# Blocks as the moving side in the compression's first layer, and decays as one product over 96 rows

## The chip, the cores and the metric

The kernel runs on one core of one Trainium2 chip. The metric is the time of the kernel on the device in microseconds (us). A core has a matrix engine (TensorE, PE in the profile; its weight loads are PEld), a vector engine (VectorE, DVE), a scalar engine (ScalarE, ACT), GpSimd (POOL), and SyncE (SP), which here issues the DMAs. Matrix products are written to PSUM, eight banks of 512 float32 columns on 128 partitions; everything else lies in SBUF.

## The reference, cut to what matters

One layer of a decoder over 1024 tokens of 1024 channels: two token mixers (native sparse attention and gated linear attention) read the same normalised input, then comes a gated feed-forward block. Two small pieces matter here. The sparse attention compresses keys and values in overlapping blocks of 32 tokens, 16 apart, for two groups, with a two-layer network:

```python
def compress_blocks(kv, pe, w1, w2):          # kv: (1, 2 groups, 1024, 64)
    ...                                       # 63 blocks of 32 x 64 for each group
    blocks = (blocks + pe).reshape(b, g, n_cmp, CMP_LEN * d)
    return jax.nn.silu(blocks @ w1) @ w2      # 2048 -> 128 -> 64
```

It is done once for keys and once for values. The linear attention has a decay for each token and key channel, from 16 numbers of low rank:

```python
log_a = jax.nn.log_sigmoid((lr_gla @ gla_gate_w2[layer] + gla_gate_b[layer])) / GLA_GATE_TAU   # 16 -> 256
```

## The kernel before

Activations lie channel-first: 128 channels on the partitions, tokens in the columns. Most products are made of two parts of each operand in float32r (a high part and what is left), as three matmuls; some small ones are plain float32, which the profile records as two passes for one matmul.

The program starts with a projection stage. `dense` turns jobs (a weight tile of 128 outputs and what to do with the result) into a list of small items, each of three matmuls for one of eight channel tiles (line 431), with items between that load the next weights: SP fetches them, ACT takes the high part (L372), POOL the rest (L373). Each job makes two halves of 512 tokens in PSUM banks of the kind `m`, of which there are two. The jobs are, in this order: a part of the linear attention's keys, `j0` (block keys), `key_job(0)` (rotated keys), `j1` (block values), `key_job(1)`. The order of the items is written out by hand in `fill.add(work[:7] + ...)`, and `fill.flush()` issues them in that order; the costs in the list play no part there. After them come two projections with tokens on the partitions (`token_proj`, L749 to L751): first `wb` (values of the linear attention), then `wa` (other values, gates and the 16 ranks `lr`). Then comes the recurrence of the linear attention (`gla_stream`, in 8 chunks), mixed with projections, and after it the attention, which a planner (`Plan`) arranges on TensorE by estimated times and in which L1210 turns the probabilities, then the merging and the feed-forward block.

TensorE runs in the order in which the program is written. The order on DVE, ACT, POOL and SP is fixed by the builder, which follows the program's order by a timeline of its own; a few stages set some of them by hand. A tile takes a free place of its kind and waits if there is none.

The compression is in `compress_job(kv)`. `fetch` loads w1 (2048 x 128 as 16 tiles), w2 and the positions. `evac` takes each half of the projection, scales it by `rbc` (the normalisation) on DVE into one tile `kst` for each group on partitions 0 to 63 (L641), and ACT copies it, shifted by one token, to partitions 64 to 127 (L644, L646), so that a column holds two neighbouring tokens. After the first half DVE also sums the positions times w1 into `pb` (L651, L653, sixteen operations). `hidden(g)` multiplies, for each of 16 pairs of places in the block, the 63 columns 16 apart (the standing side, loaded as weights) with the tile of w1 that belongs to the pair (the moving side) (L662); the second group's call adds `pb` (L666) and applies silu. Its result has the blocks on the partitions. `turned` turns it (L677, L680), and `second` makes the second layer (L686, L692).

The decays: `turn_rank(p)` turns the ranks of two token blocks on TensorE (L796), and DVE copies them to `lrT`, whose row 16 is one (L797). `decay(p)` multiplies them with `w2b`, 16 rows of weights and one of bias, in float32, one product for each block (L804), and takes the logarithm of the sigmoid. Pairs 0 and 1 are made in `token_proj(wa)`, pairs 2 and 3 in the recurrence, in chunks 1 and 3. `load_consts` loads `w2b` with the other constants.

Of the kernel before, what the change touches and what calls it, by code (L numbers as in the profile page):

```python
# [10 lines left out]
F32 = mybir.dt.float32  # L11
# [236 lines left out]
def layer_kernel(ctx, tc, a, outT):  # L248
# [86 lines left out]
    eps = cst.tile([128, 1], F32, name="eps")  # L335
    w2b = mcst.tile([17, 256], F32, name="w2b")

    def load_consts():
        load(ident, a["consts"][:, CI:CI + 128])
        load(tri, a["consts"][:, CTRI:CTRI + 128])  # L340
        load(cmul, a["consts"][:, CMUL:CMUL + 64])
        load(ggain, a["gla_norm"])
        load(w2b, a["gla_w2b"])
        V.tensor_copy(identb, ident)
        t = big("cst1")
        load(t[:, :512], a["consts"][:, CCMP:CCMP + 512])
        V.tensor_copy(cmb.rearrange("p b n -> p (b n)"), t[:, :512])
        t = big("cst2")
        load(t[:, :64 * NLV], a["consts"][:, CLEV:CLEV + 64 * NLV])
        V.tensor_copy(lev.rearrange("p b n -> p (b n)"), t[:, :64 * NLV])  # L350
# [272 lines left out]
    def compress_job(kv):  # L623
# [11 lines left out]
        def evac(p, hf):  # L635
            if hf == 0:
                d["s"] = [big("kst") for _ in range(NG)]
            for g in range(NG):
                r = slice(64 * g, 64 * g + 64)
                t, bc = d["s"][g], rbc[r, hs(hf)]  # L640
                V.tensor_mul(t[0:64, hs(hf)], p[r, :], bc)  # L641

                if hf == 0:
                    S.activation(t[64:128, 0:511], t[0:64, 1:512], AF.Copy)  # L644
                else:
                    S.activation(t[64:128, 511:1023], t[0:64, 512:1024], AF.Copy)  # L646

# [7 lines left out]

        def hidden(g):
            def fn():
                if g == 0:
                    d["ph"] = ps_m()
                dst = d["ph"][0:63, bs(g)]  # L660
                for j in range(16):
                    PE.matmul(dst, d["s"][g][:, 2 * j:2 * j + 993:16], d["w1"][j // 8][:, j % 8, :],  # L662
                              start=g + j == 0, stop=False)
                if g == 1:
                    for h in range(NG):
                        PE.matmul(d["ph"][0:63, bs(h)], ones[:, 0:63], d["b"], start=False, stop=h == NG - 1)  # L666
                    x, sg = d["h"], d["e"] = small("hx"), small("hs")
                    V.tensor_copy(x[0:63], d["ph"][0:63, :256])
                    log_sigmoid(sg[0:63], x[0:63])
                    S.activation(sg[0:63], sg[0:63], AF.Exp)  # L670
                    V.tensor_mul(x[0:63], x[0:63], sg[0:63])
            return fn

        def turned():
            ps = ps_m()
            for g in range(NG):
                PE.transpose(ps[:, 64 * g:64 * g + 63], d["h"][0:63, bs(g)], ident[0:63, 0:63])  # L677
            hd = d["hd"] = small("hd")
            P.memset(hd, 0.0)
            S.activation(hd[:, :128].rearrange("p (g n) -> p g n", g=NG)[:, :, 0:63],  # L680
                         ps[:, :128].rearrange("p (g n) -> p g n", g=NG)[:, :, 0:63], AF.Copy)

# [18 lines left out]

        return (a["w_t"][4 + kv], proj(evac)), [(2000.0, hidden(0)), (2000.0, hidden(1))], [(220.0, turned)], [(400.0, second)]

# [41 lines left out]
    def token_proj(parts, ncol, evac, after={}):  # L745
        for b in range(NB):
# [6 lines left out]
            for fn in after.get(b, []):  # L753
                fn()

    fetches = []
    j0, h0, t0, s0 = compress_job(0)
    j1, h1, t1, s1 = compress_job(1)
    lb, wb = token_weights(a["w_b"], 512, 2)
    work = dense([(a["w_t"][3], proj(lambda p, hf: scaled(kg[hf][:, 1, :], p, hf))), j0, key_job(0), j1, key_job(1)], ready=first)  # L760
    fill.add(work[:7] + [(900.0, first_roots), (0.0, load_consts), (0.0, fetches[0])] + work[7:20] + [(0.0, root_turned)] + work[20:48] + h0 + [(0.0, fetches[1])] + work[48:59] + t0
             + work[59:63] + s0 + work[63:69] + lb[:1] + work[69:74] + lb[1:2] + work[74:84] + h1 + lb[2:] + work[84:])
    fill.flush()
# [20 lines left out]
    la, wa = token_weights(a["w_a"], NA, 3)  # L784
    token_proj(wb, 512, evac_b, {0: [t1[0][1]], 2: [s1[0][1]], 4: [la[0][1]], 5: [la[1][1]], 6: [la[2][1]], 7: [la[3][1]]})


    lsg = [None] * 4
    lrT = [small("lrT") for _ in range(4)]
    for t in lrT:  # L790
        P.memset(t[0:32, :], 1.0)

    def turn_rank(p):
        ps = ps_t()
        for b in range(2):
            PE.transpose(ps[0:16, bs(b)], lr[:, 2 * p + b, :], ident)  # L796
        V.tensor_copy(lrT[p][0:16, :], ps[0:16, :256])  # L797

    def decay(p):
        z = mid("z")  # L800
        lsg[p] = mid("lsg", shape=(2, 256))
        ps = ps_d()
        for b in range(2):
            PE.matmul(ps[:, 256 * b:256 * (b + 1)], lrT[p][0:17, bs(b)], w2b, start=True, stop=True)  # L804
        S.activation(z, ps, AF.Copy)
        log_sigmoid(lsg[p].rearrange("p a b -> p (a b)"), z)
# [1144 lines left out]
```

## Time and profile before

| | us |
|---|---|
| runs, median (3 runs) | 1565.15 (1564.26 to 1566.31) |
| profiled execution, its own time | 1564.79 |
| span in its profile | 1563.0 |
| TensorE busy | 1542.0 |
| DVE busy | 1014.2 |
| ACT busy | 813.0 |
| POOL busy | 720.4 |

The profile is of one execution. The span goes from its first to its last instruction; the execution's own time has some us around it. An engine that is busy for nearly all of the span need not be at its best pace: matmuls are pipelined, and the start of one to the start of the next is what a matmul costs in a row of them. Rows of groups give: line, engine, operation, what is written from what, shapes, count, then busy time and mean of one, then the idle time ahead of them with what ended it. Rows of a timeline or a chain give: start, length, engine, line, operation, count. The granted clock of TensorE was 0.998 of full over the span.

### The profile page before, as it was taken

The page shows a single profiled execution, that of the slowest core. Times are in us where ns is not written, and L with a number is a line of the kernel's source. Part 1 is how long each engine was busy: PE and PEld are TensorE (multiplying, and loading weights), DVE is VectorE, ACT ScalarE, POOL GpSimd, SP SyncE. Part 2 cuts the span into 40 slices and gives each one's busy share as a digit, 9 for nine tenths or more (in the row PEclk, how much of TensorE's full clock was granted, in tenths as well). Part 3 has the DMA queues.
Part 4 walks back from the last instruction along what each step waited for, and adds up shares of the span by engine and source line. Part 5 has one row for each costly group of instructions (what it writes and reads, how often), then busy time and mean ns, then how long its engine had stood idle before and what let it go on. Part 6 is the DMA issues. An engine that isn't in the chain of part 4 may idle for free.

```text
span 1563.0 us, 22871 instructions
## 1 busy us (share of the span) xinstructions
PE 1542.0 (99%) x7871; PEld 1309.6 (84%) x7871; DVE 1014.2 (65%) x1788; ACT 813.0 (52%) x1615; POOL 720.4 (46%) x635
## 2 busy tenths in 40 slices
PE   9999999999999999999999999999999999999998
PEld 7888988888888888888888888888888888888887
DVE  7781487586787778777574677544444444599785
ACT  6241555575776767687653454334333334454542
POOL 6110366573223353343256510666666666555570
PEclk9999999999999999999999999999999999999999
DMA  5431212332111222221656621322222323885422
GB/s 180 139 105 55 69 51 65 119 108 78 48 58 55 77 87 72 85 88 61 200 169 229 197 88 68 121 101 102 101 101 102 101 101 108 299 320 163 141 88 108
DMA packets 109944, 180.15 MB, mean 115 GB/s; under 512 B 13426, under 2 KB 30595, under 8 KB 109828
## 3 DMA queue, kind: packets, MB, share of 16 engines
q1 hardware_dynamic: 105796, 172.25, 33.4%
q10 hardware_dynamic: 4032, 6.44, 1.1%
q8 instruction: 62, 1.02, 0.3%
q14 instruction: 54, 0.44, 0.1%
HBM read 128.57 MB, written 45.88 MB: 112 GB/s over the span
## 4 chain that ended last, share of the span: by engine, by line
PE 93%; DVE 3%; ACT 1%; issue 1%; POOL 0%; DVEq 0%; POOLq 0%; ACTq 0%
PE m L431 19%; PE d L431 11%; PE m L1494 9%; PE m L1492 9%; PE m L1493 9%; PE m L1880 5%; PE m L1882 4%; PE m L1881 4%; PE t L1210 3%; PE o L1219 3%; PE s L1130 2%; PE s L1129 2%; PE t L749 2%; PE t L750 1%; PE t L751 1%; PE t L884 1%
## 5 line engine op out<-in xcount | busy, mean ns | idle before, releaser
L373 POOL TENSOR_TENSOR wl<-wf,wh 128x512 fp32r<-128x512 f32 x106 | 146.5, 1389 | 260.7 <-ACT wh L372 237.4
L1492 PE MATMUL m<-xt,wh 128*128 128x512 f32 x412 | 160.3, 389 | 0.0
L1493 PE MATMUL m<-xt,wh 128*128 128x512 f32 x412 | 160.3, 389 | 0.0
L1494 PE MATMUL m<-xt,wl 128*128 128x512 f32 x412 | 160.3, 389 | 0.0
L1409 POOL TENSOR_TENSOR wl<-ws,wh 128x512 fp32r<-128x512 f32 x76 | 107.6, 1420 | 73.3 <-ACT wh L1408 73.3
L1188 DVE TENSOR_TENSOR ptl<-t,pth 128x512 fp32r<-128x512 f32 (+1 forms) x168 | 99.2, 597 | 42.7 <-ACT pth L1187 40.5
L1409 POOL TENSOR_TENSOR wl<-wr,wh 128x512 fp32r<-128x512 f32 x69 | 92.0, 1333 | 70.3 <-ACT wh L1408 69.3
L1408 ACT ACTIVATE wh<-wr 128x512 fp32r<-128x512 f32 x87 | 55.0, 632 | 121.3 <-POOL wl L1409 89.1
L1408 ACT ACTIVATE wh<-ws 128x512 fp32r<-128x512 f32 x76 | 48.0, 632 | 131.4 <-PE m L1493 113.8
L1187 ACT ACTIVATE pth<-t 128x512 fp32r<-128x512 f32 (+1 forms) x168 | 86.4, 519 | 53.0 <-PE t L1210 43.7
L1880 PE MATMUL m<-xb,wh 128*128 128x512 f32 x280 | 109.1, 389 | 0.3 <-DVE g L1554 0.3
L1409 POOL TENSOR_TENSOR wl<-wd,wh 128x512 fp32r<-128x512 f32 x56 | 81.9, 1465 | 59.1 <-ACT wh L1408 57.7
L1881 PE MATMUL m<-xb,wh 128*128 128x512 f32 x280 | 109.0, 389 | 0.0
L1882 PE MATMUL m<-xb,wl 128*128 128x512 f32 x280 | 108.9, 389 | 0.0
L1409 DVE TENSOR_TENSOR xb<-ar,xb 128x512 fp32r<-128x512 f32 x73 | 82.3, 1146 | 29.0 <-ACT xb L1408 29.0
L431 PE MATMUL m<-hh,wh 128*128 128x512 f32 x240 | 99.9, 416 | 0.1
L372 ACT ACTIVATE wh<-wf 128x512 fp32r<-128x512 f32 x106 | 66.1, 626 | 61.1 <-PE m L431 19.9
L1135 DVE CUSTOM_DVE_ANT_0 p<-s,qz 128x640 f32<-128x640 f32 (+7 forms) x128 | 86.3, 700 | 12.8 <-PE s L1130 12.5
L431 PE MATMUL m<-hh,wl 128*128 128x512 f32 x240 | 93.8, 391 | 0.0
L431 PE MATMUL m<-hl,wh 128*128 128x512 f32 x240 | 93.6, 390 | 0.0
L1210 PE MATMUL t<-ident,p 128*128 128x128 f32 x528 | 83.9, 275 | 8.4 <-DVE ptl L1188 6.1
L1493 PEld LDWEIGHTS m<-xt,wh 128*128 128x128 f32 x412 | 77.4, 188 | 16.2
(402 smaller groups left out, 4506.4 us busy)
## 6 DMA issues: line engine op xcount, KB each, us to landing
ar<-actd SPq DMA_DIRECT2D x77, 256.0 KB, 2.8
wf<-in_w_t SPq DMA_DIRECT2D x58, 256.0 KB, 2.8
wr<-in_w_gate SPq DMA_DIRECT2D x44, 256.0 KB, 2.8
wr<-in_w_upf SPq DMA_DIRECT2D x44, 256.0 KB, 2.7
wd<-in_w_down SPq DMA_DIRECT2D x33, 256.0 KB, 5.2
zd<-zt SPq DMA_DIRECT2D x32, 256.0 KB, 2.0
zz<-zd SPq DMA_DIRECT2D x16, 512.0 KB, 4.7
wf<-in_w_out SPq DMA_DIRECT2D x32, 256.0 KB, 3.3
```

The costliest lines, as they stand in the source:

```text
L373: P.tensor_tensor(tl, wf, f(th), OP.subtract)
L431: PE.matmul(st["p"], w, x, start=k + i == 0, stop=k == n - 1 and i == 2)
L1188: V.tensor_tensor(tl[:, :c], pt[:, :c], f(th[:, :c]), OP.subtract)
L1210: PE.transpose(pt[:, bs(2 * b + par)], self.p[par][:, bs(kb + b)], ident)
L1408: S.activation(th, src, AF.Copy)
L1409: eng.tensor_tensor(tl, src, f(th), OP.subtract)
L1492: PE.matmul(ps, wh[:, c], xh, start=first and k == 0, stop=False, skip_group_check=not first)
L1493: PE.matmul(ps, wh[:, c], xl, start=False, stop=False, skip_group_check=not first)
L1494: PE.matmul(ps, wl[:, c], xh, start=False, stop=k == MH - 1, skip_group_check=not first)
L1880: PE.matmul(dst, wh[:, c], xh, start=first and p == 0, stop=False, skip_group_check=not first)
L1881: PE.matmul(dst, wh[:, c], xl, start=False, stop=False, skip_group_check=not first)
L1882: PE.matmul(dst, wl[:, c], xh, start=False, stop=p == NP - 1, skip_group_check=not first)
```

## The change

The evacuation of a block projection writes one tile for both groups, laid out by the parity of the place in the block (partitions 0 to 63 for even, 64 to 127 for odd places), then group, pair of places (8), and sub-block (64): four strided DVE operations for each half instead of two and two ACT copies. `hidden` has w1 as the standing side and the 2 x 63 blocks of both groups as the moving side, sixteen products and one for the bias; its result has the hidden units on the partitions, so `turned` is left out, and silu ends in the tile `hd` that the second layer reads. In the list of items each first layer goes three products later; the second layer of the values goes one token block earlier.

For the decays, `w2b` gets 96 rows in float32r: the high part at rows 0 and 32, the low part at row 64, and zeros between. `lrT` gets the high part of the ranks at rows 0 and 64 (two ACT copies) and the low part at row 32 (DVE), with ones for the bias where the high part is.

```diff
     def load_consts():
...
-        load(w2b, a["gla_w2b"])
+        t = small("w2f")
+        load(t[0:17, :], a["gla_w2b"])
+        P.memset(f(w2b), 0.0)
+        for o in (0, 32):
+            V.tensor_copy(w2b[o:o + 17, :], t[0:17, :])
+        V.tensor_tensor(w2b[64:81, :], t[0:17, :], f(w2b[0:17, :]), OP.subtract)
...
         def evac(p, hf):
             if hf == 0:
-                d["s"] = [big("kst") for _ in range(NG)]
+                d["s"] = big("kst", shape=(NG, 8, 64))
             for g in range(NG):
                 r = slice(64 * g, 64 * g + 64)
-                t, bc = d["s"][g], rbc[r, hs(hf)]
-                V.tensor_mul(t[0:64, hs(hf)], p[r, :], bc)
-
-                if hf == 0:
-                    S.activation(t[64:128, 0:511], t[0:64, 1:512], AF.Copy)
-                else:
-                    S.activation(t[64:128, 511:1023], t[0:64, 512:1024], AF.Copy)
+                for o in range(2):
+                    at, bc = [x.rearrange("p (n e o) -> p o e n", e=8, o=2)[:, o] for x in (p[r, :], rbc[r, hs(hf)])]
+                    V.tensor_mul(d["s"][64 * o:64 * o + 64, g, :, 32 * hf:32 * hf + 32], at, bc)
...
-        def hidden(g):
-            def fn():
-                if g == 0:
-                    d["ph"] = ps_m()
-                dst = d["ph"][0:63, bs(g)]
-                for j in range(16):
-                    PE.matmul(dst, d["s"][g][:, 2 * j:2 * j + 993:16], d["w1"][j // 8][:, j % 8, :],
-                              start=g + j == 0, stop=False)
-                if g == 1:
-                    for h in range(NG):
-                        PE.matmul(d["ph"][0:63, bs(h)], ones[:, 0:63], d["b"], start=False, stop=h == NG - 1)
...
-        def turned():
-            ps = ps_m()
-            for g in range(NG):
-                PE.transpose(ps[:, 64 * g:64 * g + 63], d["h"][0:63, bs(g)], ident[0:63, 0:63])
-            hd = d["hd"] = small("hd")
+        def hidden():
+            n = NG * NCMP
+            ph = ps_m()[:, :n]
+            for j in range(16):
+                PE.matmul(ph, d["w1"][j // 8][:, j % 8, :], d["s"][:, :, j % 8, j // 8:j // 8 + NCMP], start=j == 0, stop=False)
+            PE.matmul(ph, d["b"], ones[:, :n], start=False, stop=True)
+            x, e, hd = small("hx")[:, :n], small("hs")[:, :n], small("hd")
+            d["hd"] = hd
             P.memset(hd, 0.0)
-            S.activation(hd[:, :128].rearrange("p (g n) -> p g n", g=NG)[:, :, 0:63],
-                         ps[:, :128].rearrange("p (g n) -> p g n", g=NG)[:, :, 0:63], AF.Copy)
+            V.tensor_copy(x, ph)
+            log_sigmoid(e, x)
+            S.activation(e, e, AF.Exp)
+            V.tensor_mul(hd[:, :128].rearrange("p (g n) -> p g n", g=NG)[:, :, 0:NCMP],
+                         x.rearrange("p (g n) -> p g n", g=NG), e.rearrange("p (g n) -> p g n", g=NG))
...
-    fill.add(work[:7] + [...] + work[7:20] + [(0.0, root_turned)] + work[20:48] + h0 + [(0.0, fetches[1])] + work[48:59] + t0
-             + work[59:63] + s0 + work[63:69] + lb[:1] + work[69:74] + lb[1:2] + work[74:84] + h1 + lb[2:] + work[84:])
+    fill.add(work[:7] + [...] + work[7:20] + [(0.0, root_turned)] + work[20:52] + h0 + [(0.0, fetches[1])] + work[52:63]
+             + s0 + work[63:69] + lb[:1] + work[69:74] + lb[1:2] + work[74:87] + h1 + lb[2:] + work[87:])
...
-    token_proj(wb, 512, evac_b, {0: [t1[0][1]], 2: [s1[0][1]], 4: [la[0][1]], 5: [la[1][1]], 6: [la[2][1]], 7: [la[3][1]]})
+    token_proj(wb, 512, evac_b, {1: [s1[0][1]], 4: [la[0][1]], 5: [la[1][1]], 6: [la[2][1]], 7: [la[3][1]]})
...
-    lrT = [small("lrT") for _ in range(4)]
+    lrT = [small("lrT", F32R) for _ in range(4)]
     for t in lrT:
-        P.memset(t[0:32, :], 1.0)
+        for o in range(3):
+            P.memset(f(t[32 * o:32 * o + 32, :]), float(o != 1))
...
-        V.tensor_copy(lrT[p][0:16, :], ps[0:16, :256])
+        for o in (0, 64):
+            S.activation(lrT[p][o:o + 16, :], ps[0:16, :256], AF.Copy)
+        V.tensor_tensor(lrT[p][32:48, :], ps[0:16, :256], f(lrT[p][0:16, :]), OP.subtract)
...
-            PE.matmul(ps[:, 256 * b:256 * (b + 1)], lrT[p][0:17, bs(b)], w2b, start=True, stop=True)
+            PE.matmul(ps[:, 256 * b:256 * (b + 1)], lrT[p][0:96, bs(b)], w2b, start=True, stop=True)
```

More of the change, by code (lines that the diff above doesn't have):

```diff
@@ L335, in layer_kernel @@
     eps = cst.tile([128, 1], F32, name="eps")
-    w2b = mcst.tile([17, 256], F32, name="w2b")
+    w2b = mcst.tile([96, 256], F32R, name="w2b")
     def load_consts():
@@ L654, in evac @@
                                            op0=OP.mult, op1=OP.add)
-        def hidden(g):
-            def fn():
-                if g == 0:
-                    d["ph"] = ps_m()
-                dst = d["ph"][0:63, bs(g)]
-                for j in range(16):
-                    PE.matmul(dst, d["s"][g][:, 2 * j:2 * j + 993:16], d["w1"][j // 8][:, j % 8, :],
-                              start=g + j == 0, stop=False)
-                if g == 1:
-                    for h in range(NG):
[L666 to L672, printed above, removed]
-        def turned():
-            ps = ps_m()
-            for g in range(NG):
-                PE.transpose(ps[:, 64 * g:64 * g + 63], d["h"][0:63, bs(g)], ident[0:63, 0:63])
-            hd = d["hd"] = small("hd")
-            P.memset(hd, 0.0)
-            S.activation(hd[:, :128].rearrange("p (g n) -> p g n", g=NG)[:, :, 0:63],
-                         ps[:, :128].rearrange("p (g n) -> p g n", g=NG)[:, :, 0:63], AF.Copy)
+        def hidden():
[6 more added lines that the diff above has]
+            d["hd"] = hd
+            P.memset(hd, 0.0)
+            V.tensor_copy(x, ph)
[3 more added lines that the diff above has]
+                         x.rearrange("p (g n) -> p g n", g=NG), e.rearrange("p (g n) -> p g n", g=NG))
         def second():
@@ L700, in second @@
                     V.tensor_tensor(v[r, 64:128], src, f(v[r, 0:64]), OP.subtract)
-        return (a["w_t"][4 + kv], proj(evac)), [(2000.0, hidden(0)), (2000.0, hidden(1))], [(220.0, turned)], [(400.0, second)]
+        return (a["w_t"][4 + kv], proj(evac)), [(3700.0, hidden)], [(400.0, second)]
     swap = list(range(32))
@@ L756, in layer_kernel @@
     fetches = []
-    j0, h0, t0, s0 = compress_job(0)
-    j1, h1, t1, s1 = compress_job(1)
+    j0, h0, s0 = compress_job(0)
+    j1, h1, s1 = compress_job(1)
     lb, wb = token_weights(a["w_b"], 512, 2)
     work = dense([(a["w_t"][3], proj(lambda p, hf: scaled(kg[hf][:, 1, :], p, hf))), j0, key_job(0), j1, key_job(1)], ready=first)
-    fill.add(work[:7] + [(900.0, first_roots), (0.0, load_consts), (0.0, fetches[0])] + work[7:20] + [(0.0, root_turned)] + work[20:48] + h0 + [(0.0, fetches[1])] + work[48:59] + t0
-             + work[59:63] + s0 + work[63:69] + lb[:1] + work[69:74] + lb[1:2] + work[74:84] + h1 + lb[2:] + work[84:])
+    fill.add(work[:7] + [(900.0, first_roots), (0.0, load_consts), (0.0, fetches[0])] + work[7:20] + [(0.0, root_turned)] + work[20:52] + h0 + [(0.0, fetches[1])] + work[52:63]
+             + s0 + work[63:69] + lb[:1] + work[69:74] + lb[1:2] + work[74:87] + h1 + lb[2:] + work[87:])
     fill.flush()
```

## The prediction

> **What bounds the kernel now.** First the page's busy times and its chain of work that ended last:
>
> ```profile
> span 1563.0 us, 22871 instructions
> ...
> PE 1542.0 (99%) x7871; PEld 1309.6 (84%) x7871; DVE 1014.2 (65%) x1788; ACT 813.0 (52%) x1615; POOL 720.4 (46%) x635
> ...
> PE 93%; DVE 3%; ACT 1%; issue 1%; POOL 0%; DVEq 0%; POOLq 0%; ACTq 0%
> ```
>
> TensorE is busy for 99% of the span and holds 93% of the chain, so matmul time taken out anywhere should come off the end, unless a wait fills the hole. Next the same chain between 60 and 112 us, where both compressions run (start, length, what):
>
> ```profile
> 66.97 0.09 issue
> 67.05 0.94 PE m L431 x3
> 67.99 1.29 issue
> 69.28 7.23 PE m L662 x64
> ...
> 76.94 6.34 PE m L431 x27
> 83.28 0.26 PE m L677 x2
> ...
> 86.72 12.97 PE m L431 x57
> 99.69 0.56 issue
> 100.26 7.23 PE m L662 x64
> ```
>
> The reader should see two blocks of 64 passes (L662; a float32 matmul is recorded as two passes), each behind a gap, and that this stage is TensorE work end to end: even its shadows are 1.29 and 0.56 us. L431 goes at 12.97 / 57 = 0.2275 us a pass of 512 columns.
>
> **First layer.** Before, the block is the standing side (63 columns) and w1 moves (128 columns): 16 products for each of two groups. After, w1 stands and 2 x 63 = 126 columns move, so 16 products do both groups, and one bias product replaces two: 34 passes instead of 68. What is a pass with 128 standing and 128 moving columns worth? The row of the decay levels has it:
>
> ```profile
> 199.99 0.89 PE t L884 x8
> ...
> 209.48 1.06 PE d L804 x4
> ```
>
> 0.89 / 8 = 0.111 us, against 7.23 / 64 = 0.113 for the old form (the second row, of a decay, is used below): the pace follows the moving columns. From the start of the block to the next projection it takes 76.94 - 69.28 = 7.66 us; after, 34 x 0.111 = 3.8. Saved 3.9 for each of two, **7.7 us**. All of it was on the path.
>
> **The turn** of the hidden activations goes away (the result already stands hidden-first). Timeline of TensorE around the first, and the chain's row of the second:
>
> ```profile
> 82.90 0.39 PE L431 MATMUL m<-hh,wl 128*128 128x512 f32 x1
> 83.22 0.33 PE L677 MATMUL m<-ident,hx 63*128 63x63 f32 x2
> 83.48 0.50 PE L431 MATMUL m<-hh,wh 128*128 128x512 f32 x1
> 83.81 0.39 PE L431 MATMUL m<-hl,wh 128*128 128x512 f32 x1
> ```
>
> ```profile
> 118.34 0.26 PE m L677 x2
> ```
>
> Two L431 steps would take 0.455; 83.81 - 82.90 = 0.91, so the turn with its restart costs 0.455, twice: **0.9 us**. The ACT copy behind it goes too, off the path. The second layer, now at most 11 items behind the first, waits for copy, Abs, Exp, Ln, two DVE operations: six of some 0.4 us, against ten projection steps of 3 x 0.2275 = 6.8 us. Covered; if DVE is late, TensorE stands for the rest. The second one runs a token block earlier than before but still over two blocks later than its first layer; nothing.
>
> **Decays.** Four pairs, each two float32 products (four passes), become two float32r products:
>
> ```profile
> 170.52 0.30 PE L751 MATMUL t<-th,hl 128*128 128x296 f32 x1
> 170.75 1.13 PE L804 MATMUL d<-w2b,lrT 17*128 17x256 f32 x4
> 171.81 0.41 PE L749 MATMUL t<-th,hh 128*128 128x296 f32 x1
> 172.05 0.30 PE L750 MATMUL t<-tl,hh 128*128 128x296 f32 x1
> ```
>
> From 170.52 two float32r steps of 0.137 would reach 170.79; the pair costs 172.05 - 170.79 = 1.26. A float32r pass of 256 columns is half of L431's, 0.115; two are 0.23. Saved 1.0 in each of the two pairs of the token projection. The two in the recurrence stand between float32 products and keep a switch, so 0.8 each; but at the last one DVE, not TensorE, carries the chain right behind it:
>
> ```profile
> 237.05 0.56 DVE at L886
> 237.66 1.05 DVE xq L853 x3
> ```
>
> There I count half: 2.0 + 0.8 + 0.4 = **3.2 us** (bounds 2.0 and 3.6).
>
> **The two gaps, and the new layout.** The hidden product needs a bank of the pair m, and its last user is the rotated key, whose evacuation (krt) is queued on DVE behind the block evacuation (kst) and the bias sum (pb):
>
> ```profile
> 65.24 0.68 DVE L641 TENSOR_TENSOR kst<-m,rbc 64x512 f32<-64x512 f32 x1
> ...
> 66.21 0.69 DVE L641 TENSOR_TENSOR kst<-m,rbc 64x512 f32<-64x512 f32 x1
> 66.94 1.51 DVE L653 SCALAR_TENSOR_TENSOR pb<-w,pe,pb 128x128 f32<-128x128 f32 x4
> 68.48 0.69 DVE L565 TENSOR_TENSOR krt<-m,rbc 128x512 f32<-128x512 f32 x1
> ...
> 96.76 2.68 DVE L653 SCALAR_TENSOR_TENSOR pb<-w,pe,pb 128x128 f32<-128x128 f32 x7
> 99.46 0.69 DVE L565 TENSOR_TENSOR krt<-m,rbc 128x512 f32<-128x512 f32 x1
> ```
>
> krt ends at 69.17 and 100.15, the blocks start 0.1 later: that is what "issue" hides. The change puts the product three steps (3 x 0.68 = 2.04 us) later, so these waits of 1.29 and 0.56 go, if DVE is not much slower. But DVE now does four strided pieces of 256 columns for each half instead of two of 512 (the eight shifted ACT copies of 0.63 go; they are off the path). Contiguous rows of those sizes:
>
> ```profile
> L641 DVE TENSOR_TENSOR kst<-m,rbc 64x512 f32<-64x512 f32 x8 | 5.5, 687 | 0.2
> ...
> L668 DVE COPY hx<-m 63x256 f32<-63x256 f32 x2 | 0.8, 417 | 3.1 <-PE m L666 3.1
> ```
>
> That is 0.147 + 1.055 ns a column: four pieces 1.67 against 1.37, 0.3 more a half. At the first block kst then ends at 66.9 + 0.6 = 67.5, so the step at 67.05 starts at 67.6; four steps later, 70.35, krt (69.8) is done. Counted back by 2.04 that is 68.3 instead of 69.28: 1.0 gained. Late next is the bank of that step, by 0.8. At the second block DVE is all but full, as this row of the stretch from 83 to 104 us has it (busy time of PE, PEld, DVE, ACT, POOL):
>
> ```profile
> 83.00:104.00 21.00, 20.43 (x109) 17.07 (x108) 19.43 (x39) 7.85 (x14) 3.32 (x7) 1.00 0.50 161
> ```
>
> Between the evacuation of one rotated key and of the next, DVE will have 4.9 (rotation, seven operations of 0.7), 0.6 (compressed keys), 3.3 (kst, two halves), 3.7 (weight parts), 6.1 (bias sum, sixteen of 0.38) and 0.7 (krt): 19.3 us. TensorE has 16 + 8 + 4 projection steps and the second layer in that time, 28 x 0.68 + 0.4 = 19.5. It fits with nothing over, so I count 0.4 of 0.56. Together **1.4 us**. The upper end is 1.9 (all gaps gone). For the lower I take the slowest strided neighbour, the decay levels' operation over 256 columns (its columns: smallest, median, largest):
>
> ```profile
> L853 DVE TENSOR_TENSOR xq<-xx,qz x56: 408/673/1501, 186.6 to 284.5; 128x256 f32<-128x256 f32 x56
> ```
>
> With its median, 0.67, a half costs 1.3 more, 2.6 a block: krt at 71.8 and, at the second, 2 us past TensorE. Term: -0.7 - 1.6 = -2.3. I take 1.4: the pieces read PSUM and SBUF like L641 and L668.
>
> **Small parts.** The constants get three DVE operations of some 0.35 and a POOL memset (POOL is idle there). The DVE queue has these holes before the blocks:
>
> ```profile
> 40.50 1.29 DVE L590 TENSOR_TENSOR ssl<-ssq,ssh 128x512 fp32r<-128x512 f32 x2 [0.56 <-ACT ssh L589]
> ...
> 57.91 0.29 DVE L651 TENSOR_SCALAR pb<-w,pe 128x128 f32<-128x128 f32 x1 [2.08 <-DMA w<-in_cmp_w]
> ```
>
> In the second hole they cost nothing, in the first they push the roots by about 0.5: **-0.3**. No DMA is added; the second block's weights are asked for after one weight half more, so that half is earlier on SP. Twelve memsets instead of four are on an idle POOL. Turning the ranks takes two ACT copies and a DVE subtraction instead of a DVE copy. In the token projection a whole block lies between turn and decay. In the recurrence ACT's queue behind the turn is
>
> ```profile
> 206.75 1.07 ACT L848 ACTIVATE xx<-xx 128x1024 f32<-128x1024 f32 x1 [0.43 <-POOL xx L846]
> 207.85 1.06 ACT L849 ACTIVATE xx<-xx 128x1024 f32<-128x1024 f32 x1
> ```
>
> In the 0.43 hole the copies push the exponentials by about 0.4; behind both they end at 209.7 and the decay (209.48 in the chain above) comes some 0.9 later. Twice, between 0 and 0.9, partly covered: **-0.5**.
>
> **Sum.** 7.7 + 0.9 + 3.2 + 1.4 - 0.3 - 0.5 = 12.4. The profiled execution took 1564.79 us, so 1552.4; the median of the runs is 0.36 higher, so 1552.8.
>
> **Rivals.**
> A. *DVE carries the compression stage* (chance 0.14). Strided pieces at 0.67 turn the 1.4 into -2.3: 1556.5. For it: DVE is busy for 19.43 of those 21 us. Against it: 64-byte steps are read by L662's weight loads without a loss of pace. [...]
> B. *The recurrence gives the decay part back* (0.07). If DVE and ACT set the pace there, the decays keep only the 2.0 of the token projection and the new copies cost 1.8: 12.4 - 1.2 - 1.3 = 9.9, 1555.3; with the exponentials late in both chunks by a further 1, 1557.
> C. *The passes do not get fewer in time* (0.03): were a pass paced by its standing columns (126 to 128 instead of 63), the first part would be nothing: 1560.5. L884's row speaks against it.
> D. *Slower* (0.03; and 0.05 for no change by the same way). Only TensorE's order is written by hand; the queues of DVE, ACT, POOL and SP are ordered by the builder's own timeline, and one early difference can reorder them in the attention. There TensorE already waits:
>
> ```profile
> PE t L1210 <- DVE ptl L1188: 6.1, 10, 2.7
> ```
>
> To end slower this 6.1 must grow by 12.4 + 3.1 = 15.5, to over 21 us; by 10 to 15 for no change. Nothing in the changed lines touches that stage.
>
> **How the numbers follow.** My case has 0.68, own range 1550 to 1555 (from all upper ends, 14 to 15, to 10). With A, B and C faster has 0.92; same 0.05; slower 0.03; 0.2% (3.1 us) is about what a measurement here tells from no change. For 8 in 10 I go from 1549 to 1558.5: A and B inside, C and D out, and below, all gaps gone and an eighth less attention wait.
>
> **What would show it.** In the changed profile: 32 passes at 0.11 in each block, the blocks 3.6 long; no turn; two decay passes of about 0.115; no gap over 0.3 ahead of the blocks; strided kst pieces near 0.42. Pieces near 0.7 with a krt that ends late show A; a TensorE wait at L804 on DVE's lrT, or longer waits at L884, show B; longer waits at L1210 show D and would make the prediction wrong.

## The result, and the profile after

The changed kernel takes 1556.5 us (median of 4 runs, 1555.1 to 1557.4) against 1565.6 for the kernel before on the same chip: ratio 0.9942, 95% interval 0.9925 to 0.9960. Run once more in a later group it took 1556.4, ratio 0.9943 (0.9929 to 0.9957). So the gain is 9.1 us where 12.4 were forecast. The profiled execution took 1557.39 us, 7.4 less than the one before. One of the nine executions of old_places took 3125.2 us; it is left out of the range given there and moves the median by 0.1.

The page of the changed kernel, its span, busy times and the shares of its chain of work that ended last:

```profile
span 1555.5 us, 22722 instructions
...
PE 1530.7 (98%) x7791; PEld 1301.1 (84%) x7791; DVE 1016.1 (65%) x1799; ACT 808.7 (52%) x1613; POOL 721.6 (46%) x644
...
PE 87%; DVE 5%; ACT 1%; issue 1%; DMA 0%; POOL 0%; DVEq 0%; ACTq 0%; POOLq 0%
```

TensorE lost 11.3 us of busy time (1542.0 to 1530.7), close to the forecast's 11.8 of first layer, turns and decays. But the span shrank by only 7.5: TensorE's share of the chain fell from 93% to 87%, and DVE's rose from 3% to 5%. New waits ate the difference. The chain between 60 and 108 us shows where (start, length, what):

```profile
67.12 0.59 DVE kst L647
67.72 0.58 DVE kst L647
68.32 0.59 DVE kst L647
68.93 0.35 DVE pb L654
69.32 0.58 DVE kst L647
70.04 2.98 PE m L436 x12
73.02 3.57 PE m L661 x32
...
98.98 0.70 DVE krt L570
99.73 3.84 PE m L661 x32
...
103.79 2.78 PE m L436 x12
```

Before, TensorE carried this stretch from end to end. Now the path runs through DVE's queue in front of each block: through the strided pieces (kst) and the bias sum (pb) at the first, through the rotated key (krt) at the second. The blocks themselves are what was forecast, 32 passes in some 3.8 us. TensorE's timeline at the places of the waits (in brackets: idle time and what ended it):

```profile
63.71 0.47 PE L436 MATMUL m<-hh,wh 128*128 128x512 f32 x1 [1.70 <-DVE kst L647]
...
70.04 0.47 PE L436 MATMUL m<-hh,wh 128*128 128x512 f32 x1 [0.60 <-DVE kst L647]
...
72.86 3.73 PE L661 MATMUL m<-kst,w 128*128 128x126 f32 x32
...
76.57 0.48 PE L436 MATMUL m<-hh,wh 128*128 128x512 f32 x1
...
99.73 3.84 PE L661 MATMUL m<-kst,w 128*128 128x126 f32 x32 [0.37 <-DVE krt L570]
```

From the block's start to the next projection it is 76.57 - 72.86 = 3.71. The gap of 1.29 ahead of the first block is gone, and waits of 1.70 and 0.60 have come in the projection steps ahead of it. The pieces themselves, grouped by shape (smallest, median, largest ns) in the first block's stretch:

```profile
L647 DVE TENSOR_TENSOR kst<-m,rbc x8: 568/578/589, 61.2 to 69.3; 64x256 f32<-64x256 f32 x8
```

0.578 us where the forecast had 0.42. The decays, in the token projection:

```profile
163.83 0.40 PE L796 MATMUL d<-w2b,lrT 96*128 96x256 f32 x2
164.07 0.30 PE L738 MATMUL t<-th,hh 128*128 128x296 f32 x1
```

Two passes in 164.07 - 163.83 = 0.24, as forecast (0.23), and the step behind them takes 0.30, where the one behind the old pair took 0.41. Last, TensorE's waits between 175 and 365 us (in all, times, longest):

```profile
PE t L876 <- DVE at L878: 1.8, 3, 0.9
PE t L876 <- POOL xx L849: 0.8, 1, 0.8
PE s L1100 <- DVE qr L572: 0.8, 1, 0.8
```

Before, the masked copies (at) made TensorE wait once for 0.7, and the rows for xx and qr were not there.

**A ledger.** The same instruction of TensorE can be found in each trace: the first pass of each block (69.28 before, 72.86 after), the first step of the token projection, each chunk's first, and so on. The difference of their starts says how much was gained up to there. The two blocks stand 9 passes later in the order (9 x 0.2275 = 2.05 us), which is taken out. Gain against before in us, by stretch:

| stretch | forecast | after | after, again | layer_only | act_pieces | decays_only | decays_ordered | best1 |
|---|---|---|---|---|---|---|---|---|
| start to first block (first gap, constants) | 1.0 - 0.3 | -1.5 | -0.4 | 0.2 | 1.3 | -1.0 | -0.1 | 1.4 |
| first block to second (layer, turn, second gap) | 4.7 | 4.1 | 4.1 | 4.1 | 4.2 | 0.0 | 0.0 | 4.2 |
| second block to token projection (layer) | 3.9 | 3.8 | 3.8 | 3.8 | 3.8 | 0.0 | 0.0 | 3.8 |
| token projection to chunk 0 (turn 0.45, decays 2.0) | 2.45 | 2.5 | 2.5 | 0.5 | 2.5 | 2.0 | 2.0 | 2.5 |
| chunk 0 to chunk 5 (decays 1.2, copies -0.5) | 0.7 | -0.3 | -0.3 | 0.0 | -0.3 | -0.3 | 1.3 | 1.4 |
| chunk 5 to the attention's first | 0 | -1.35 | -1.4 | -1.4 | -1.4 | -0.5 | -0.45 | -1.4 |
| attention's first to the end | 0 | 0.3 | 0.6 | 1.4 | 1.6 | -0.2 | 1.8 | 0.5 |

The middle rows came as forecast. The first, the fifth and the sixth did not. The last is one profiled execution against another: 1.2 us of its differences is the granted clock of TensorE, which fell once, to some 0.5, near 750 us in before, after, after again and best1 and not in the other four (shown at the end of this document).

### The profile page after: what moved, and what is told of

The parts are those of the page before. It is cut to its first block, busy times and chain, and to the rows that moved or that the text cites. A ratio compares the mean times of both kernels' runs of the same rounds, so it can differ in the third digit from the quotient of the medians.

```text
span 1555.5 us, 22722 instructions
## 1 busy us (share of the span) xinstructions
PE 1530.7 (98%) x7791; PEld 1301.1 (84%) x7791; DVE 1016.1 (65%) x1799; ACT 808.7 (52%) x1613; POOL 721.6 (46%) x644
## 4 chain that ended last, share of the span: by engine, by line
PE 87%; DVE 5%; ACT 1%; issue 1%; DMA 0%; POOL 0%; DVEq 0%; ACTq 0%; POOLq 0%
PE m L436 16%; PE d L436 11%; PE m L1486 9%; PE m L1484 9%; PE m L1485 9%; PE m L1872 5%; PE m L1874 5%; PE m L1873 5%; PE t L1202 3%; PE o L1211 3%; PE s L1122 2%; PE s L1121 2%; PE t L740 1%; PE t L738 1%; PE t L739 1%; PE t L876 1%
```

## The experiments

### Each half alone

layer_only is the changed kernel with w2b, lrT and the two decay products of each pair as before; decays_only is the kernel before with these alone changed.

```
- w2b = mcst.tile([96, 256], F32R, name="w2b")       # layer_only, against after
+ w2b = mcst.tile([17, 256], F32, name="w2b")
...
- PE.matmul(ps[:, 256 * b:256 * (b + 1)], lrT[p][0:96, bs(b)], w2b, start=True, stop=True)
+ PE.matmul(ps[:, 256 * b:256 * (b + 1)], lrT[p][0:17, bs(b)], w2b, start=True, stop=True)
```

> Changed kernel with the decays as before; only the compression is new. Theory Q (the strided evacuation pieces, 0.58 us each instead of the forecast 0.42, make DVE late, so TensorE waits for banks): the first token projection starts some 6.8 us earlier than before (6.3 in the changed kernel, plus 0.5 of the constants), with the waits of about 1.7 and 0.6 us for kst still there; the decays then gain nothing, so about 6 to 7 us faster than before, near 1559. Theory R (the missing part is lost in the recurrence, to the new copies of the ranks on ACT): no loss between the chunks, and the end is as far ahead as the token projection's start.

Measured: 1557.7 (1556.4 to 1557.7), ratio 0.9945 (0.9932 to 0.9959): 8.5 faster, more than theory Q's 6 to 7. In its trace the two waits for kst are one of 1.1, and nothing is lost between the chunks.

> Kernel before with the decay part alone. Forecast terms: four decays 1.0, 1.0, 0.8, 0.8 us shorter, constants 0.3 to 0.5 lost. Theory Q: the terms hold (each pair 0.8 to 1.0 shorter in the trace), of which up to 1.9 us are given back behind chunk 0 and the last decay by the order on DVE: 1.3 to 3 us faster in all, near 1563. Theory R: the two decays of the recurrence and the copies together lose what they gain; 1 us or less.

Measured: 1566.7 (1564.3 to 1570.0) against 1566.2, ratio 1.0005 (0.9995 to 1.0015). The layer brings nearly all of the gain, the decays in this form nothing (theory R's 1 us or less), although each of their four products got shorter as forecast: the ledger has 2.0 gained in the token projection, and 1.0 lost up to the first block, 0.3 in the recurrence and 0.5 behind it.

### What a piece costs

flat_pieces reads both operands of the strided product in one run of 256 columns, so that the blocks hold other tokens and only the time says something. one_side does so with one operand only: in the first compression the factors rbc (so that only the PSUM operand is strided), in the second the projection (so that only rbc, in SBUF, is).

```
- at, bc = [x.rearrange("p (n e o) -> p o e n", e=8, o=2)[:, o] for x in (p[r, :], rbc[r, hs(hf)])]
+ at, bc = [x.rearrange("p (o e n) -> p o e n", e=8, o=2)[:, o] for x in (p[r, :], rbc[r, hs(hf)])]   # flat_pieces
```

> Changed kernel, but each evacuation piece reads 256 neighbouring columns of the projection and of the scale instead of every 16th: the compressed keys and values are of wrongly ordered tokens, only the time is of interest. Same instructions in the same order. Theory Q: pieces take 0.42 instead of 0.58, the wait ahead of the rotated keys' first half falls from 1.7 to about 1.1 (what is left is the late start of the bias sum on DVE), the next from 0.6 to 0, the second block's waits are gone: 1.5 to 2 us ahead of the changed kernel at the first token projection. Theory L (DVE is held by the load of w1 ahead of the bias sum, the pieces do not matter): at most 0.7.

Measured: 1555.3 (1554.2 to 1556.5), ratio 0.9931 (0.9919 to 0.9944). Its pieces:

```profile
L647 DVE TENSOR_TENSOR kst<-m,rbc x16: 409/422/428, 62.2 to 94.6; 64x256 f32<-64x256 f32 x16
```

In its profile the first block starts no earlier than in the change (72.87 against 72.86), and the token projection 0.65 earlier, not the 1.5 to 2 of theory Q. But the weights w1 came later there: the first bias operation (L652), which waits for them, started at 61.08 instead of 59.58. From its start to the first block it takes 13.28, 13.24 and 13.15 us with strided pieces (after, after_again, layer_only) and 11.79 and 11.86 with pieces of 0.42 (flat_pieces, one_side). From the first block to the second, flat_pieces gains 4.65 over before, the forecast's 4.7, where the change has 4.1.

> The changed kernel, but in each of its two block evacuations only one of the two operands is read at the step of 16 floats (64 bytes): in the first (keys) the projection in PSUM, in the second (values) the factors rbc in SBUF; the other operand is read in one run of 256 columns, so the tokens are paired wrongly (the blocks hold the keys or values times factors of other tokens). Both strided: 0.582 us a piece in the changed kernel; both contiguous: 0.43. Theory S (only the SBUF operand pays for its step): first block 0.43, second 0.58. Theory P (only the PSUM operand pays): first 0.58, second 0.43. Theory E (either step alone sets the pace, the slower stream decides): 0.58 in both. Theory H (the steps add): some 0.50 in both.

The groups of the first compression's pieces, then of the second's, in one_side (one profiled execution):

```profile
L648 DVE TENSOR_TENSOR kst<-m,rbc x8: 408/422/428, 60.8 to 68.6; 64x256 f32<-64x256 f32 x8
...
L648 DVE TENSOR_TENSOR kst<-m,rbc x8: 578/592/599, 86.3 to 94.4; 64x256 f32<-64x256 f32 x8
```

0.422 contiguous is the forecast's 0.42; the difference is the step. And it is the SBUF operand alone that pays: 0.592 with rbc strided, 0.422 with the PSUM operand strided at the same 64 bytes (theory S of the expectation). The step costs 0.17 us on 0.422, 40%. Both steps flattened, the kernel's median is 1.1 us lower than the second run of the change in another group of runs; the intervals overlap, so this difference in time is a hint, and the pieces' duration and the two stretches of the trace are what is shown.

### How much DVE time matters

act_pieces does the product in one DVE operation of 128 x 512 a half and lets ScalarE, busy for 0.63 us of the 9 from 61 to 70 in the change, spread it into the four pieces.

```
+ t = mid("kf")
+ V.tensor_mul(t, p, rbc[:, hs(hf)])
...
- V.tensor_mul(d["s"][64 * o:64 * o + 64, g, :, 32 * hf:32 * hf + 32], at, bc)
+ S.activation(d["s"][64 * o:64 * o + 64, g, :, 32 * hf:32 * hf + 32], src, AF.Copy)
```

> Changed kernel, but one DVE operation of 128 x 512 evacuates both groups and ACT spreads the four pieces. DVE has 0.69 us a half instead of 2.33. Theory Q: no wait for kst or krt at TensorE in the compression stage; the first token projection starts 2.5 to 3 us earlier than in the changed kernel, near 103.5, and the whole is as much faster, near 1553.5. Theory L: DVE still waits for w1 ahead of the first piece where the bias sum stands first; no more than 0.7. Against both: ACT pieces slower than 1 us would make the first layer wait for kst from ACT.

Measured: 1554.4 (1553.2 to 1555.1), ratio 0.9925 (0.9912 to 0.9937). Tile kf in the first compression's stretch, with its readers:

```profile
L648 ACT ACTIVATE kst<-kf x8: 635/646/653, 57.4 to 67.6; 64x256 f32<-64x256 f32 x8
L644 DVE TENSOR_TENSOR kf<-m,rbc x2: 681/686/691, 56.7 to 64.9; 128x512 f32<-128x512 f32 x2
```

DVE has 0.69 a half instead of 2.33. TensorE's waits between 36 and 115 us are then these two:

```profile
PE o L600 <- DVE ssl L595: 1.0, 1, 1.0
PE m L662 <- issue: 0.8, 1, 0.8
```

The waits on kst (2.3 in the profiled change) are gone, and the ledger's first row rises to 1.3, above the forecast. So the loss in this row was DVE's time in the first compression, and it came off the end: the intervals of the two ratios overlap, but only the slowest of the five executions (1555.13) comes up to the fastest of the change's nine (1555.11).

### Does the weights' landing set it?

In the change the bias sum waits in front of the pieces for the weights w1, and the profiled execution had a late landing. after_again is the changed kernel once more; w1_first asks for w1 ahead of the constants.

```
- (0.0, load_consts), (0.0, fetches[0])
+ (0.0, fetches[0]), (0.0, load_consts)
```

> The changed kernel once more, beside the other three. Both theories: 8 to 9.5 us faster than before. In its trace the time at which w1 lands (from its issue 4.7 to 6.7 us in the runs so far) and the wait for kst ahead of the rotated keys' first half should go together: theory L says that this wait is the landing plus the fixed work behind it, theory Q that most of it is there at any landing.

> Changed kernel, but the first block's w1 is asked for ahead of the constants, so it lands some 10 us before the bias sum needs it; the pieces stay strided (0.58 us). The builder also moves the three operations on the decay weights behind the first bias sums. Theory L (the landing of w1 holds DVE, and with it kst): the wait of 1.7 us ahead of the rotated keys' first half is gone, the first block starts near 70.5 and the first token projection near 104; about 2 us faster than the changed kernel. Theory Q (DVE has too much work with strided pieces): of the two kst waits at least 1 us stays, and the second block's waits of 0.2 and 0.4 too.

Measured: 1556.4 (1555.3 to 1556.6), ratio 0.9943 (0.9929 to 0.9957), and 1556.3 (1555.6 to 1557.8), ratio 0.9945 (0.9931 to 0.9959): no difference in time. In after_again the wait on kst was 1.1 instead of 2.3, the first bias operation started at 58.45 instead of 59.58 and the first block at 71.69 instead of 72.86, so the landing explains 1.2 us between two profiled executions of one kernel. Asked for earlier, the weights did not remove the wait (1.5 in w1_first). That run is no clean test, though: in the freed time the builder put 2.1 us of work on the constants (the casts and the split of w2b, L347 to L355) among DVE's pieces. What tells the two apart is the stretch above: the first block comes 13.2 us behind the first bias operation with strided pieces and 11.8 with contiguous ones. So the landing sets when DVE's work begins and the pieces how long it takes, and both count.

### What the later place is worth

The prediction priced the move of the two blocks by the gaps that stood in front of them, 1.29 and 0.56. old_places puts them back; act_old_places does the same in act_pieces.

```
- work[20:52] + h0 + [(0.0, fetches[1])] + work[52:63] ... work[74:87] + h1 + lb[2:] + work[87:]
+ work[20:48] + h0 + [(0.0, fetches[1])] + work[48:63] ... work[74:84] + h1 + lb[2:] + work[84:]
```

> The changed kernel with the hidden products put back in the places that they had before (after 48 and 84 items of the list instead of 52 and 87). Theory Q (the DVE queue carries the evacuations' banks; TensorE is late by the same whichever item stands there): the wait of 2.3 us on kst shrinks by what the earlier product hides, but the product then waits for krt, 1.5 to 2.5 us at L661 in the first block and about 1 in the second; the sum of the two blocks' waits grows by 0.5 to 1.5 us and the time is 1556.5 to 1558. Rival F (the later place alone brought the forecast's full 1.4): the time grows by 1.9 (1.29 + 0.56 back), 1558.3 or more. Rival N (the place is worth nothing): 1556.4.

Measured: 1561.7 (1559.5 to 1563.9), ratio 0.9974 (0.9964 to 0.9984): 5.3 us over the change. More than half of what the change gains hangs on the place. TensorE's waits between 36 and 115 us in old_places:

```profile
PE m L661 <- DVE krt L570: 3.7, 2, 2.4
PE m L436 <- DVE kst L647: 1.5, 1, 1.5
PE o L600 <- DVE ssl L595: 0.9, 1, 0.9
```

That is 2.5 us more on kst and krt than in the change (5.2 against 2.7), and in the profiled execution there is a second price. Busy times by stretch (PE, PEld, DVE, ACT, POOL, then the granted clock, DMA share, GB/s), and the first block in the timeline:

```profile
66.00:72.00 6.00, 3.60 (x15) 2.36 (x13) 5.60 (x14) 0.00 (x0) 0.00 (x0) 0.97 0.83 281
72.00:80.00 8.00, 7.68 (x38) 7.55 (x39) 4.33 (x9) 1.59 (x4) 0.00 (x0) 0.60 0.06 24
```

```profile
70.14 0.47 PE L436 MATMUL m<-hh,wh 128*128 128x512 f32 x1 [1.47 <-DVE kst L647]
...
72.31 6.73 PE L661 MATMUL m<-kst,w 128*128 128x126 f32 x32 [1.24 <-DVE krt L570]
```

Behind two waits of 1.47 and 1.24 with one step of 0.7 between them, the granted clock was 0.60 in the next 8 us, and the 32 passes took 6.73 instead of 3.84: 2.9 us, as much as the waits. In the change the waits of 1.70 and 0.60 lie 6 us apart, and over the same stretch, from 66 to 80 us, the clock stays at 1.00. In old_places neither wait is longer than 1.47, and TensorE is idle for 2.7 us out of 3.6 ahead of the fall. This is one execution, at 1563.9 the slowest of that range. The sum of the idle time does not settle it alone: act_old_places, below, has one wait of 2.78 (95.28 to 98.06), and behind it the clock stays at 1.00. Of the theories, Q had the mechanism (krt behind the strided pieces) but not the size, since none of them had the clock.

> act_pieces (one DVE operation a half, ScalarE spreads the pieces) with the hidden products in the places that they had before the change (after 48 and 84 items). old_places lost 5 us to the changed kernel: its products waited 3.7 us for krt behind the strided pieces, and the granted clock fell to 0.50 behind the waits. Theory Q (the later place only covers DVE's strided pieces): with 1.4 us less DVE work a block than even before the change, the products find krt done in the old places too, there is no wait over 0.5 at L661 and no fall of the clock, and the time is that of act_pieces within 0.7, 1554 to 1555.1. Rival G (the place is worth the old gaps of 1.29 and 0.56 by itself, since krt is late for another reason): waits of 1.3 and 0.6 at L661 and 1556.2. Rival W (it is worth as much as in old_places): 1559.

Measured: 1558.9 (1557.3 to 1561.1), ratio 0.9957 (0.9945 to 0.9969): 4.6 over act_pieces. Theory Q was wrong here; the time is that of W. The longest of the waits in this kernel, and ScalarE's and DVE's queues ahead of the second block:

```profile
PE m L662 <- issue: 2.8, 1, 2.8
```

```profile
92.22 2.63 ACT L648 ACTIVATE kst<-kf 64x256 f32<-64x256 f32 x4 [2.88 <-DVE kf L644]
94.87 1.15 ACT L363 ACTIVATE th<-wt 128x512 fp32r<-128x512 f32 x2
...
95.54 0.69 DVE L364 TENSOR_TENSOR tl<-wt,th 128x512 fp32r<-128x512 f32 x1 [1.54 <-ACT th L363]
...
97.27 0.68 DVE L570 TENSOR_TENSOR krt<-m,rbc 128x512 f32<-128x512 f32 x1
```

The wait of 2.8 ends when krt is done (97.95, the block starts at 98.06). krt stands in DVE's queue behind a weight part (tl) that waits 1.54 for ScalarE, which is busy with the pieces until 94.85. act_pieces has the same 1.56 there; the later place covers all but 0.8 of the wait, and the old one doesn't. So the place covers whatever delays krt, in one kernel DVE's pieces and in the other a queue behind ScalarE, not the pieces alone. In this execution 3.2 us are lost up to the token projection (106.72 against 103.53), 2.7 of them in waits (4.5 against 1.8). The spans differ by 4.1, and 1.2 of that is the fall of the clock near 750 us, which act_pieces' profiled execution has not (0.83 from 750 to 760 us against 1.00). What the medians' 4.6 is made of is open.

### The order of the queues

decays_ordered is decays_only with two moves: the split of w2b stands behind the other constants, and the gate's reciprocal is kept behind the recurrence. best1 has the same two moves on top of act_pieces. act_layer is act_pieces with the decays as before.

```
  t = big("cst1") ...                        # the other constants first
+ t = small("w2f") ... V.tensor_tensor(w2b[64:81, :], t[0:17, :], f(w2b[0:17, :]), OP.subtract)
...
- S.activation(gate, gz, AF.Exp, scale=-1.0); V.tensor_scalar(gate, ...); V.reciprocal(gate, gate)
  ...                                        # the recurrence
+ S.activation(gate, gz, AF.Exp, scale=-1.0)
+ tc.keep_in_program_order(V.tensor_scalar(gate, gate, 1.0, None, op0=OP.add))
+ tc.keep_in_program_order(V.reciprocal(gate, gate))
```

> Kernel before with the decay part, but the split of the decay weights placed behind the other constants and the two gate operations on DVE (1.3 us for the reciprocal) put behind the recurrence. Theory O (the decay part is worth its 3.7 us, and the run with it alone gave it back because DVE ran other work first: 1.0 to 1.5 ahead of the roots, 1.1 behind chunk 0, 0.7 behind the last decay): ahead of before by 0 at the first decay, 2.0 at chunk 0, 2.9 to 3.5 at chunk 4, and 2 to 3 us faster in all. Theory R (the recurrence is bound by DVE, ACT and POOL whatever the order): of 2.0 at chunk 0 no more than 1 is left at chunk 2; 1 us faster at most.

Measured: 1561.6 (1560.2 to 1564.8), ratio 0.9978 (0.9968 to 0.9987); decays_only was 1.0005. Two of the rows of waits between 36 and 260 us, decays_only's and then decays_ordered's:

```profile
PE t L892 <- DVE at L894: 1.8, 3, 0.9
PE o L600 <- DVE ssl L595: 1.0, 1, 1.0
```

```profile
PE t L892 <- DVE at L894: 0.7, 1, 0.7
PE o L600 <- DVE ssl L595: 0.2, 1, 0.2
```

1.1 and 0.8 us of waits go, and the ledger gains 0.9 up to the first block and 1.6 in the recurrence. The kernel is 3.6 faster than before, more than theory O's 2 to 3. The medians are 5.1 apart, in different groups of runs; the half of that which the first six rows don't show isn't explained. What happened in the recurrence is seen in DVE's timeline of the change, and, second, of the kernel before:

```profile
183.24 1.34 DVE L924 RECIPROCAL gz<-gz 128x192 f32<-128x192 f32 x1
184.50 0.93 DVE L878 COPY_PREDICATED at<-lev,t 128x256 f32<-128x256 uint8 x2
```

```profile
191.81 0.44 DVE L886 COPY_PREDICATED at<-lev,t 128x256 f32<-128x256 uint8 x1
192.14 1.33 DVE L932 RECIPROCAL gz<-gz 128x192 f32<-128x192 f32 x1
193.40 0.93 DVE L886 COPY_PREDICATED at<-lev,t 128x256 f32<-128x256 uint8 x2
```

Before, one masked copy went ahead of the gate's reciprocal; after, the builder's order has the reciprocal first, and the levels' turns wait 1.8 in all instead of 0.7. Neither line was edited. The decay part moved them: layer_only, without it, keeps the 0.7. That it did so by making the builder's own timeline think something else ready is argued, not shown.

> Changed kernel with all three repairs: one evacuation on DVE with ACT spreading the pieces, the decay weights split behind the other constants, the gate operations behind the recurrence. Theories Q and O together: the first token projection starts near 102.5 to 103, chunk 4 near 225, and the whole is 13 to 15 us faster than before, near 1552. Theory R: no faster than the version with ACT pieces alone (1554.4).

Measured: 1553.3 (1551.0 to 1553.9), ratio 0.9921 (0.9908 to 0.9934): below both kernels, 11.9 under the 1565.2 of before. That is about what the change was forecast to bring, and less than the 13 to 15 expected of this run.

> The first layer with one DVE operation a half and the pieces spread by ScalarE (as in act_pieces), but the decays as before the change. It prices the decay part in a kernel whose compression stage has no DVE wait. Theory O (the decay part is worth its forecast only when the constants and the reciprocal stand behind): act_layer is within 1 us of act_pieces (1554.4, unordered decays), so 1554 to 1555.5, and about 3.6 us over best1 less what the ordering of the constants gains by itself, 1554 to 1557. Rival R (decays_only lost its gain to the old layer's place alone, and in the new one the decays bring the forecast 3.2 - 0.3 - 0.5 = 2.4 even unordered): 1556.8. From the landmarks: the start of the decays 9.4 to 9.8 us earlier than before in both, then no change through the recurrence under both.

Measured: 1556.5 (1556.4 to 1556.9), ratio 0.9942 (0.9928 to 0.9955). Against act_pieces the unordered decays are then worth 2.1 us, and against best1 the ordered ones 3.2 (2.9 in the ledger up to the attention's first score). The time is that of rival R (1556.8) and not theory O's 1554 to 1555.5, but the ratios' intervals overlap, and by the ledger the unordered decays are worth only 1.1 at that point, where decays_only had 0.3. So in this layer the decays do pay, even in the bad order; how much is not settled.

## Why the prediction was right or wrong

The time fell inside the range, and the sign and the bulk were right, but the forecast gain was a third too high and the time lies outside the range given for the main case (1550 to 1555).

- **First layer, 7.7: right.** 3.71 and 3.81 from block to next projection against 7.6 before; the 34 passes take 3.71 / 34 = 0.109 each with 126 moving columns, and rival C is out. The rows of layer_only and of the change agree to 0.05.
- **Turn, 0.9: right where it can be seen.** The second turn lay in the token projection, which gained 0.5 in layer_only (no new decays; forecast 0.45). The first lies in one row with the layer and the gap.
- **Decays, 3.2: right for the passes.** 2.0 in the token projection; with the order held in decays_ordered, 1.3 from chunk 0 to chunk 5 (forecast 0.7 after the copies' -0.5). The ScalarE copies that were to cost 0.5 show in no wait.
- **Gaps and new layout, 1.4: mis-sized; it measured about 0.** The step that failed is "I take 1.4: the pieces read PSUM and SBUF like L641 and L668": those rows are contiguous, and the 64-byte step on the SBUF operand adds 0.17 to a piece, 0.7 to a half. layer_only, free of the constants, gained 0.2 where 1.0 was forecast ahead of the first block (w1 landed as in before: first bias operation at 58.02 and 57.91), and 4.1 where 4.7 was from first to second, 1.4 less in all. With contiguous pieces the 4.7 came, and the stretch to the first block was 1.4 shorter. Rival A had the mechanism (DVE carries the stage). What was said against it, that TensorE's weight loads read 64-byte steps without loss (0.113 us a pass against 0.111), bore on another engine. That its price of 1556.5 equals the result is chance: its piece of 0.67 was too dear, and half of the loss lay elsewhere. The row that the 0.67 came from, L853, is no measure of a step: in the trace of before its 15 operations beside which no GpSimd instruction runs took 0.41 to 0.42, and all those over 0.5 have one beside them (last section).
- **The price of the place was wrong by a factor of two and more**, unseen in the sum. It was taken as the gaps before, 1.29 and 0.56; put back in the new kernel the old places cost 5.3. At the first block krt ends later than before (72.26 instead of 69.17, w1 having come 1.9 later too), and in the profiled execution the clock fell on top of it (0.60 over 72 to 80 us). At the second the faster block brings TensorE there earlier than DVE follows: in act_old_places TensorE is ready at 95.28 instead of 99.69, krt done at 97.95 instead of 100.15.
- **Constants, -0.3: mis-sized.** They went into the first of the two holes, ahead of ssl; the step to the first block is 0.5 worse than layer_only's in after_again and 1.7 in the profiled change, but w1 landed 0.4 and 1.6 later there, so these don't price them. act_pieces is 0.6 worse than act_layer, and decays_only loses 1.0, as much as TensorE's wait for ssl there. Behind the other constants it is 0.1.
- **Recurrence, 0.7 net: it came out at -0.3.** Rival B's give-back came in part (its price was -1.8), but not from ScalarE's copies or a bound on DVE: it is the reciprocal's place, and decays_ordered and best1 undo it.
- **Not in the prediction at all:** 1.4 lost between chunk 5 and the attention's first score in every kernel with the new layer, 0.8 of it a wait for the last rotated query (qr); the kernels with the decays alone lose 0.5. The second block ends 250 us earlier. Before, the same product (L1108) started at 361.54, ahead of that query's evacuation (361.74), so it did not wait for it. No run was made for it, and the cause stays open.
- **Rival D** did not come: the attention and what follows gained 0.3 to 0.6 instead.

## What to carry to other kernels

Price a DVE operation by a row with the same step of each operand, not only the same size: here the step of the SBUF operand alone was worth 40% (0.592 against 0.422 us), and that of the PSUM operand nothing (0.422). When TensorE's work in front of a full engine gets shorter, ask whether the other engine's next result comes earlier too; if not, the item must move later in the order. Look at the clock behind the waits as well: here it was 0.60 behind 2.7 us of them in one profiled execution and 1.00 behind 2.78 in another. Where a builder orders the queues by its own timeline, a shorter operation can reorder lines that nobody touched: look for a long operation (here a reciprocal of 1.33 us) that jumped ahead of a short one on the path, and hold it back.

## What was not expected of the hardware

The fallen clock behind 2.7 us of waits, shown above (0.60 over 8 us), came with 2.9 us more in the 32 passes, as much as the waits. Whether it falls is not set by the wait alone. In the attention all 14 traces have the same wait of TensorE, 2.72 to 2.74 us, for ptl. Before, and then act_pieces, with the clock (third number from the end) of the stretch behind it:

```profile
757.27 0.70 PE L1210 MATMUL t<-ident,p 128*128 128x128 f32 x4 [2.73 <-DVE ptl L1188]
757.70:761.10 3.40, 3.40 (x19) 3.40 (x17) 1.49 (x3) 1.29 (x3) 0.00 (x0) 0.51 0.98 365
```

```profile
747.47 0.66 PE L1203 MATMUL t<-ident,p 128*128 128x128 f32 x4 [2.72 <-DVE ptl L1181]
747.90:751.30 3.40, 3.37 (x28) 3.13 (x26) 1.93 (x4) 1.58 (x3) 0.00 (x0) 1.00 0.99 356
```

At this wait the clock goes to 0.50 in ten of the traces (for 3.4 us, in w1_first for 6.8) and stays at 1.00 in four: layer_only, act_pieces, decays_only, decays_ordered. Each of these four gains 1.2 us on before within the next 10 us, the kernels with one short fall less than 0.2, and w1_first loses 1.2. What decides it no run here shows. It fits that of layer_only's five executions two took 1556.4 and 1556.6 and three 1557.7. So a difference of 1.2 us between two profiled executions need not come from the edit.

Further, steps of the bias sum on DVE, whose operands lie in SBUF, took longer beside a GpSimd subtraction. This one, 0.35 us as a rule, took 1.41 in the change, while GpSimd's row beside it ran (DVE's timeline, then GpSimd's):

```profile
59.90 1.41 DVE L654 SCALAR_TENSOR_TENSOR pb<-w,pe,pb 128x128 f32<-128x128 f32 x1
```

```profile
59.86 1.30 POOL L378 TENSOR_TENSOR wl<-wf,wh 128x512 fp32r<-128x512 f32 x1 [6.61 <-ACT wh L377]
```

In the 14 traces 31 of these steps took over 0.6 us, and each lies beside such a GpSimd operation for all but 0.15 us of its time at most; none of the shorter ones does for more than 0.3. The pieces, with one operand in PSUM, run at 0.58 beside the same kind of GpSimd operation. And the first bias operation, which waits for the load of w1, started anywhere from 57.9 to 61.1 us in the 12 traces in which it waits for that load and the load stands behind the constants in the program.
